# Adding the residual by transfers of GpSimd in the output product of a hybrid encoder block

## The chip, the cores and the metric

The kernel runs on one core of a Trainium2 chip. The metric is the device time of one execution in microseconds. A core has a matrix engine (TensorE, PE in the profile, with its weight loads as PEld), a vector engine (VectorE, DVE), a scalar engine (ScalarE, ACT), GpSimd (POOL) and SyncE (SP), which here only issues transfers. Each engine runs its own queue of instructions in order; semaphores hold an instruction back until what it needs is done. Transfers run on 16 DMA engines that all queues share.

## The reference

The computation is one layer of a hybrid encoder on 256 rows of 4096 numbers, all in float32. The parts that matter here are the last ones:

```
h = h + concat([y_a, y_c]) @ w_out                       # h was x, the input
gate = sigmoid(rms_norm(h, ple_norm_g) @ w_ple_gate + b_ple_gate)
h = h + gate * (p @ w_ple)
return rms_norm(h, final_g)
```

`y_a` (attention) and `y_c` (convolution) are the two halves of 2048 columns each. `rms_norm` divides a row by the root of its mean square, so it needs the sum of squares of each whole row of `h`. The kernel keeps `h` itself unscaled in the gate product and multiplies by the row's factor (`r_h` in the kernel) afterwards.

## The kernel before

The 256 rows are two halves of 128 (`h` = 0, 1 in the code), and the columns are eight blocks of 512. A product is computed for two column blocks at a time, which is called a group here: `w_out` has four groups, `w_ple_gate` has four. One group accumulates over 32 row blocks of the weights, two at a time, in 16 pairs. Every float32 operand is split into a high and a low part, and each product is three matrix products of TensorE (high by high, low by high, high by low), each 128 x 128 by 128 x 512. The high part of the weights is a cast on ScalarE (L204, `wh` or `uh`), the low part a subtraction on VectorE (L205, `wl` or `ul`). Tiles for the parts rotate through three buffers each, and weights (`wt`, 512 KB each, loaded by SyncE at L403) through five.

`mixed_product` treats some pairs in a plain manner (24 matrix products) and others in Strassen's manner with seven products for eight (21 matrix products, plus sums of weights, L426 to L431, on VectorE). A list of units gives the order of the pairs: `dense` is `1 0* 3 2* 5 4* ...`, where a star marks a pair done with seven products; `late` has all plain pairs of odd number first. The seven products need helper accumulators (`P1`, `P5`, `P6`, `P7`) in four PSUM banks beside the four accumulators `acc[h][j]`. After the last starred pair, `on_helpers` combines the helpers: `helper_sums` (L467 to L471) copies `P1` and makes three sums. After the last pair, the four quarters are finished from `acc`.

Work that can wait is put in a list, `later`. `fill(n)` takes `n` entries from it after each pair; `fills` sets `n` (2 in `w_out`, 4 in the gate product). `ahead` makes operands for the next product: `h_ahead` transposes finished blocks of `h` on TensorE (L170), splits them into high (L156, ScalarE) and low parts (L157, VectorE), and is called once before the last pair of `w_out` and then, pair by pair, in the first gate group.

A scheduler places the instructions: the order in the code gives priorities and the dependences, and each engine's queue is the scheduler's order, not the code's. Queues are in order on the chip.

In the output product, L1049 loads the two blocks of `x` into the tiles `hc` on SyncE's queue; these tiles are slots that the `y` blocks held before. `on_helpers` adds the helpers onto `hc` (L1057 to L1061), and L1070 adds the accumulators. `square_sum` (L500, ScalarE) sums the squares of each finished quarter through `later`. After the fourth group the list is emptied, and `rstd_of` (L504 and L138 on VectorE, L139 on GpSimd) makes `r_h`. Its first reader is L1091, in the `on_helpers` of the first gate group.

Of the kernel before, what the change touches and what calls it, by code (L numbers as in the profile page):

```python
# [10 lines left out]
F32 = mybir.dt.float32  # L11
F32R = mybir.dt.float32r
AF = mybir.ActivationFunctionType
ALU = mybir.AluOpType
AX = mybir.AxisListType

P = 128
NB = 512
# [7 lines left out]
def hybrid_block(  # L26
# [23 lines left out]
    nc = tc.nc  # L50
    _, T, D = x.shape
    NH = T // P
# [15 lines left out]
    def pool(name, bufs, stack=ctx, side=0, **kw):  # L68
        return stack.enter_context(tc.tile_pool(name=name, bufs=bufs, side=sides[side], **kw))

    cpool = pool("cpool", 1)
    act = pool("act", 8)
# [63 lines left out]
    def rsqrt(dst, src, n):  # L136

        nc.vector.tensor_scalar(dst, src, 1.0 / n, EPS, ALU.mult, ALU.add)  # L138
        nc.gpsimd.tensor_tensor(dst, dst, mhalf[:, : dst.shape[1]], ALU.pow)  # L139
# [40 lines left out]
    later = deque()  # L180

    def fill(n):
        for _ in range(min(n, len(later))):
            later.popleft()()
# [141 lines left out]

    def mixed_product(
        w, col, lhs, comb, order, on_helpers, ahead=None, fills=(0,), on_begin=None, apart=NB,
        left=(), begin=None,
    ):  # L330
# [64 lines left out]
        for n, (pair, seven) in enumerate(order):  # L395
# [59 lines left out]
            if n == last_seven:  # L455
                on_helpers(helper)
# [4 lines left out]
    tt, stt = nc.vector.tensor_tensor, nc.vector.scalar_tensor_tensor  # L461
    QUARTERS = ((0, 0), (1, 0), (0, 1), (1, 1))

    def helper_sums(helper, z):


        nc.scalar.copy(z[1][0], helper["P1"])  # L467
        tt(z[1][0], helper["P6"], z[1][0], ALU.add)
        tt(z[0][1], helper["P5"], z[1][0], ALU.add)
        tt(z[1][0], helper["P7"], z[1][0], ALU.add)  # L470
        tt(z[1][1], helper["P5"], z[1][0], ALU.add)  # L471

    def sum_tiles():

        t = [spool.tile([P, NH, NB], F32, tag="stage", name="z") for _ in range(2)]
        return t, [[t[j][:, h] for j in range(2)] for h in range(NH)]

    def scaled_pair(w, col, apart, order, r, fills, **kw):

        t, z = [], []  # L480

        def on_helpers(helper):
            for dst, src in zip((t, z), sum_tiles()):
                dst.extend(src)
            nc.scalar.activation(z[0][0], helper["P1"], AF.Identity, scale=r[:, :1])
            helper_sums(helper, z)
            for h, j in QUARTERS[1:]:
                nc.scalar.activation(z[h][j], z[h][j], AF.Identity, scale=r[:, h : h + 1])

        c = mixed_product(w, col, xT, xS, order, on_helpers, fills=fills, apart=apart, **kw)  # L490
        for h, j in QUARTERS:
            stt(  # L492
                z[h][j], c[h][j], r[:, h : h + 1], z[h][j],
                ALU.mult, ALU.subtract if j else ALU.add,
            )
        return t
# [5 lines left out]
    def rstd_of(partial, n, name):  # L502
        r = cpool.tile([P, partial.shape[1]], F32, name=name)
        nc.vector.tensor_reduce(r, partial, AX.X, ALU.add)  # L504
        rsqrt(r, r, n)
        return r
# [433 lines left out]
    for c0, order in zip(range(0, CW // NB, 2), point):  # L940
        row = broadcast_row(b_pw, c0 * NB, 2 * NB, tag="stage")
        rows = [row[:, j * NB : (j + 1) * NB] for j in range(2)]
        ys, z = [], []
# [4 lines left out]
        def on_helpers(helper):  # L948
            y_tiles()
            z.extend([ys[j][:, h, :] for j in range(2)] for h in range(NH))  # L950
            tt(z[0][0], helper["P1"], rows[0], ALU.add)
            helper_sums(helper, z)
            for h, j in QUARTERS[1:]:
                tt(z[h][j], z[h][j], rows[j], ALU.subtract if j else ALU.add)

        acc = mixed_product(w_pw[0], c0 * NB, uS, uC, order, on_helpers)
# [35 lines left out]
    def before_last(make):  # L992

        return lambda pair: make(0) if pair == dense[-1][0] else None
# [29 lines left out]
    hs, hT, hS = [], [], []  # L1024
# [17 lines left out]
                embedding()  # L1042

    ssq_h = cpool.tile([P, NH, D // NB], F32, name="ssq_h")
    for c0 in range(0, D // NB, 2):
        for j in range(2):
            hc = act.tile([P, NH, NB], F32, tag="act", name="hc")
            c = c0 + j
            nc.sync.dma_start(  # L1049
                hc, x[0, :, c * NB : (c + 1) * NB].rearrange("(h q) n -> q h n", q=P)  # L1050
            )
            hs.append(hc)

        def on_helpers(helper):
            _, z = sum_tiles()
            h00, h01, h10, h11 = (hs[c0 + j][:, h, :] for h in range(NH) for j in range(2))
            tt(h00, helper["P1"], h00, ALU.add)  # L1057
            helper_sums(helper, z)
            tt(h01, h01, z[0][1], ALU.subtract)
            tt(h10, h10, z[1][0], ALU.add)  # L1060
            tt(h11, h11, z[1][1], ALU.subtract)  # L1061

        acc = mixed_product(
            w_out[0], c0 * NB, yT, yS, dense if c0 else late, on_helpers,
            ahead=y_ahead if c0 == 0 else before_last(h_ahead) if c0 + 2 == D // NB else None,
            fills=(2,),
        )
        for h, j in QUARTERS:
            hc = hs[c0 + j][:, h, :]
            tt(hc, acc[h][j], hc, ALU.add)  # L1070
            later.append(partial(square_sum, ssq_h[:, h, c0 + j : c0 + j + 1], hc))
    fill(len(later))
    r_h = rstd_of(ssq_h, D, "r_h")


    n_f = D // NB
# [47 lines left out]
    c0 = n_f - 2  # L1124
    _, z = sum_tiles()
# [17 lines left out]
    def on_helpers(helper):  # L1143
# [4 lines left out]
    acc, add_left = mixed_product(  # L1148
        w_ple_gate[0], c0 * NB, hT, hS, final, on_helpers, fills=(4,), on_begin=on_begin,
        left=[None] * 3 + [kept] * 3,  # L1150
    )
# [119 lines left out]
```

## Time and profile before

| What | Value |
|---|---|
| Median of three runs | 2040.47 us (2038.33 to 2040.82) |
| Profiled execution | 2039.1 us, span 2037.3 us |
| Busy in the span | TensorE 2019.6 us, VectorE 1887.9, ScalarE 1200.8, GpSimd 8.1 |
| Bytes moved | 412.29 MB, 202 GB/s on average |
| Granted TensorE clock | 0.998 |

The span is the time from the first to the last instruction of the profiled execution, 1.8 us shorter than its device time. In the profile's views a line such as `L370 PE MATMUL acc<-wh,big_t 128*128 128x512 f32 x3788 | 1172.1, 391` names the source line, the engine, the operation, the output and the inputs, shapes and the count, and then the busy time in us and the mean of one in ns. In a timeline the first number is the start in us from the span's start, the second the duration, and in brackets stands the idle time of the engine ahead of the instruction with what ended it. Matrix products overlap in the pipeline, so the start to start distance says more than the duration. A row of the view by stretches gives for each engine the busy time and the number of instructions, then the granted clock, the busy share of the DMA engines and the GB/s that they moved.

### The profile page before, as it was taken

To read this page: it belongs to the slowest core of one execution; us is meant where nothing else is said; L and a number is where in the kernel's file an instruction comes from. 1 tells how busy PE (TensorE), PEld (TensorE's weight loads), DVE (VectorE), ACT (ScalarE), POOL (GpSimd) and SP (SyncE) were. 2 spreads that over 40 slices of the span, in tenths; PEclk is the share of its full clock that TensorE was granted. 3 is DMA by queue.
4 is the path that set the end of the run, shared out by engine and by line. 5 is a ranking of instruction groups with operands and counts; after the bars stand their busy time and mean duration, and the time that the engine had idled before them with its cause. 6 is when DMAs were issued, how large, how long until landed. Compare 5 with 4: busy or idle time off the path is not lost.

```text
span 2037.3 us, 26041 instructions
## 1 busy us (share of the span) xinstructions
PE 2019.6 (99%) x9106; PEld 1659.5 (81%) x9106; DVE 1887.9 (93%) x2688; ACT 1200.8 (59%) x1559; POOL 8.1 (0%) x19
## 2 busy tenths in 40 slices
PE   9999999999999999999999999999999999999997
PEld 7888888877888888888888888888888888888876
DVE  7999999799989998868899999999999999999998
ACT  7655546554565546676555656676565666655555
POOL 0000000000000000000000000000000000000000
PEclk9999999999999999999999999999999999999999
DMA  8666665666656665655666666676666656666765
GB/s 295 188 200 204 204 187 165 202 191 189 184 185 204 201 188 183 186 184 199 190 216 204 197 216 199 219 238 204 214 201 205 214 185 208 198 221 205 235 208 179
DMA packets 161853, 412.29 MB, mean 202 GB/s; under 512 B 12974, under 2 KB 16190, under 8 KB 161722
## 3 DMA queue, kind: packets, MB, share of 16 engines
q1 hardware_dynamic: 161072, 409.80, 63.3%
q8 instruction: 71, 1.16, 0.2%
q10 hardware_dynamic: 650, 0.84, 0.1%
q14 instruction: 60, 0.49, 0.1%
HBM read 406.39 MB, written 4.19 MB: 202 GB/s over the span
## 4 chain that ended last, share of the span: by engine, by line
PE 86%; DVE 10%; issue 2%; DMA 1%; ACT 1%; POOLq 0%; POOL 0%; ACTq 0%; DVEq 0%
PE acc L370 61%; PE acc_P L370 15%; PE acc L218 7%; DVE wl L205 4%; DVE cv L677 3%; DMA wt<-in_w_in_dram 1%; PE tmp_ps L170 1%; DVE ul L205 1%; PE tmp_ps L867 0%; PE tmp_ps L849 0%; ACT wh L204 0%; PE acc L358 0%; PE tmp_ps L834 0%; DVE z L492 0%; PE tmp_ps L872 0%
## 5 line engine op out<-in xcount | busy, mean ns | idle before, releaser
L370 PE MATMUL acc<-wh,big_t 128*128 128x512 f32 x3788 | 1172.1, 391 | 0.6 <-DVE z L988 0.3
L204 ACT CAST wh<-wt 128x1024 fp32r<-128x1024 f32 (+1 forms) x737 | 715.8, 982 | 543.0 <-PE acc L370 330.6
L205 DVE TENSOR_TENSOR wl<-wt,wh 128x1024 fp32r<-128x1024 f32 (+1 forms) x737 | 825.4, 1132 | 65.0 <-ACT wh L204 60.1
L370 PEld LDWEIGHTS acc<-wh,big_t 128*128 128x128 f32 x3788 | 708.4, 188 | 146.5 <-issue 0.6
L370 PE MATMUL acc<-wl,big_t 128*128 128x512 f32 x1894 | 731.1, 391 | 1.0 <-DVE wl L205 1.0
L370 PEld LDWEIGHTS acc<-wl,big_t 128*128 128x128 f32 x1894 | 355.2, 188 | 76.7 <-DVE wl L205 3.1
L677 DVE SCALAR_TENSOR_TENSOR cv<-uT,dw,cv 128x255 f32<-128x255 f32 (+23 forms) x480 | 204.9, 467 | 1.1
L204 ACT CAST uh<-ub 128x1024 fp32r<-128x1024 f32 x122 | 128.5, 1054 | 126.2 <-DVE ub L431 102.7
L218 PE MATMUL acc<-wh,big_t 128*128 128x512 f32 x560 | 173.1, 390 | 0.0
L204 ACT CAST uh<-ua 128x1024 fp32r<-128x1024 f32 x122 | 128.7, 1055 | 71.7 <-DVE ua L427 63.5
L205 DVE TENSOR_TENSOR ul<-ub,uh 128x1024 fp32r<-128x1024 f32 x122 | 149.0, 1221 | 8.8 <-ACT uh L204 7.8
L370 PE MATMUL acc_P<-uh,big_t 128*128 128x512 f32 x504 | 154.4, 392 | 0.0
L205 DVE TENSOR_TENSOR ul<-ua,uh 128x1024 fp32r<-128x1024 f32 x122 | 148.9, 1220 | 0.4 <-ACT uh L204 0.2
L218 PEld LDWEIGHTS acc<-wh,big_t 128*128 128x128 f32 x560 | 104.8, 188 | 21.4
L370 PEld LDWEIGHTS acc_P<-uh,big_t 128*128 128x128 f32 x504 | 93.3, 188 | 22.2 <-ACT uh L204 3.7
L218 PE MATMUL acc<-wl,big_t 128*128 128x512 f32 x280 | 109.1, 390 | 0.0
L426 DVE TENSOR_TENSOR ua<-wt 128x512 f32<-128x512 f32 x122 | 83.9, 688 | 25.9 <-DMA wt<-in_w_in_dram 19.0
L370 PE MATMUL acc_P<-ul,big_t 128*128 128x512 f32 x252 | 96.8, 392 | 0.0
L427 DVE TENSOR_TENSOR ua<-wt 128x512 f32<-128x512 f32 x122 | 83.7, 686 | 3.9 <-DMA wt<-in_w_in_dram 3.0
L431 DVE TENSOR_TENSOR ub<-ub,wt 128x512 f32<-128x512 f32 x122 | 83.8, 687 | 1.0
L430 DVE TENSOR_TENSOR ub<-ua,wt 128x512 f32<-128x512 f32 x122 | 83.7, 686 | 0.3
L370 PE MATMUL acc<-uh,big_t 128*128 128x512 f32 x244 | 75.4, 390 | 0.0
(241 smaller groups left out, 1523.0 us busy)
## 6 DMA issues: line engine op xcount, KB each, us to landing
wt<-in_w_in_dram SPq DMA_DIRECT2D x447, 512.0 KB, 4.0
wt<-in_w_out_dram SPq DMA_DIRECT2D x128, 512.0 KB, 4.2
wt<-in_w_ple_gate_dram SPq DMA_DIRECT2D x128, 512.0 KB, 4.2
wt<-in_w_pw_dram SPq DMA_DIRECT2D x32, 512.0 KB, 4.5
hc<-in_x_dram SPq DMA_DIRECT2D x8, 512.0 KB, 5.8
wt<-in_w_ple_dram SPq DMA_DIRECT2D x8, 512.0 KB, 4.2
xin<-in_x_dram SPq DMA_DIRECT2D x7, 512.0 KB, 8.2
out_dram<-hc SPq DMA_DIRECT2D x12, 256.0 KB, 2.4
```

The lines of the kernel that those rows point to most:

```text
L170: nc.tensor.transpose(pt[:, i * T + h * P : i * T + (h + 1) * P], src[:, h, b * P : (b + 1) * P], ident,)
L204: nc.scalar.copy(wh[:, :kc, :], wt[:, :kc, :]),
L205: nc.vector.tensor_tensor(wl[:, :kc, :], wt[:, :kc, :], wh[:, :kc, :].bitcast(F32), ALU.subtract),
L218: nc.tensor.matmul(acc, a, b[:, k, :], start=kb == 0 and kind == 0, stop=kb == kblocks - 1 and kind == 2,)
L370: nc.tensor.matmul(banks[name], a, b, start=name not in begun, stop=final and ends[name] == n and kind == 2 and not (left and name in "P2 ...
L426: plus(ua[:, 0], w0[:, 0], w0[:, 1])
L427: plus(ua[:, 1], w0[:, 1], w1[:, 1])
L430: plus(ub[:, 0], ua[:, 0], w1[:, 1])
L431: plus(ub[:, 1], ub[:, 0], w1[:, 0])
L677: nc.vector.scalar_tensor_tensor(cv[:, i, PAD - k :], uT[:, i, : T + k - PAD], dw[:, b, k : k + 1], cv[:, i, PAD - k :], ALU.mult, ALU.add,)
```

## The change

The residual `x` is no longer loaded ahead. `on_helpers` and the final additions write the product itself into the tiles `hc`: `P1` is copied there by ScalarE (L1053), `helper_sums` writes the other quarters there, and L1062 joins the accumulators. When both halves of a block are finished, a transfer issued by GpSimd (L1064) adds the block of `x` from DRAM onto the tile; there are eight such transfers of 512 KB. The squares go into `later` behind eight empty entries, so that at two entries for each pair they come four pairs later in the code. The list isn't emptied after the fourth group; the squares of its blocks, eight more empty entries and the making of `r_h` (`scale_h`) are taken from the list in the first gate group, four entries for each pair.

```diff
+    def x_columns(c):
+        return x[0, :, c * NB : (c + 1) * NB].rearrange("(h q) n -> q h n", q=P)
+
     for c0 in range(0, D // NB, 2):
-        for j in range(2):
-            hc = act.tile([P, NH, NB], F32, tag="act", name="hc")
-            c = c0 + j
-            nc.sync.dma_start(
-                hc, x[0, :, c * NB : (c + 1) * NB].rearrange("(h q) n -> q h n", q=P)
-            )
-            hs.append(hc)
+        hs.extend(act.tile([P, NH, NB], F32, tag="act", name="hc") for _ in range(2))
+        z = [[hs[c0 + j][:, h, :] for j in range(2)] for h in range(NH)]
 
         def on_helpers(helper):
-            _, z = sum_tiles()
-            h00, h01, h10, h11 = (hs[c0 + j][:, h, :] for h in range(NH) for j in range(2))
-            tt(h00, helper["P1"], h00, ALU.add)
+            nc.scalar.copy(z[0][0], helper["P1"])
             helper_sums(helper, z)
-            tt(h01, h01, z[0][1], ALU.subtract)
-            tt(h10, h10, z[1][0], ALU.add)
-            tt(h11, h11, z[1][1], ALU.subtract)
...
         for h, j in QUARTERS:
-            hc = hs[c0 + j][:, h, :]
-            tt(hc, acc[h][j], hc, ALU.add)
-            later.append(partial(square_sum, ssq_h[:, h, c0 + j : c0 + j + 1], hc))
-    fill(len(later))
-    r_h = rstd_of(ssq_h, D, "r_h")
+            tt(z[h][j], acc[h][j], z[h][j], ALU.subtract if j else ALU.add)
+        for j in range(2):
+            nc.gpsimd.dma_start(hs[c0 + j], x_columns(c0 + j), accum_op=ALU.add)
+        later.extend([lambda: None] * 8)
+        for h, j in QUARTERS:
+            later.append(partial(square_sum, ssq_h[:, h, c0 + j : c0 + j + 1], z[h][j]))
+    r_h = cpool.tile([P, NH], F32, name="r_h")
+
+    def scale_h():
+        nc.vector.tensor_reduce(r_h, ssq_h, AX.X, ALU.add)
+        rsqrt(r_h, r_h, D)
+
+    later.extend([lambda: None] * 8 + [scale_h])
```

## The prediction

> **What bounds the kernel now.** I read the page first, then busy times by stretch, then TensorE's timeline.
>
> ```profile
> span 2037.3 us, 26041 instructions
> PE 2019.6 (99%) x9106; PEld 1659.5 (81%) x9106; DVE 1887.9 (93%) x2688; ACT 1200.8 (59%) x1559; POOL 8.1 (0%) x19
> ```
>
> ```profile
> core 0: us, PE busy (x) PEld busy (x) DVE busy (x) ACT busy (x) POOL busy (x), PEclk, DMA share, GB/s
> 1312.00:1360.00 48.00, 48.00 (x241) 40.17 (x240) 44.72 (x82) 33.53 (x57) 0.00 (x0) 1.00 0.70 225
> ```
>
> ```profile
> 1664.00:1668.40 4.40, 4.40 (x26) 3.77 (x26) 4.10 (x9) 3.86 (x11) 0.00 (x0) 1.00 0.01 4
> ...
> 1412.00:1660.00 248.00, 248.00 (x1104) 205.50 (x1103) 237.81 (x283) 149.91 (x180) 0.00 (x0) 1.00 0.63 206
> ```
>
> The w_out product, which the change touches, runs from about 1312 to 1663. Between 1412 and 1660 TensorE is busy 248.00 of 248.00 us, VectorE 237.81 and ScalarE 149.91. A busy TensorE may still hide small waits, so I look at its starts:
>
> ```profile
> 1416.51 0.61 PE L370 MATMUL acc<-wh,big_t 128*128 128x512 f32 x2
> ...
> 1421.95 0.61 PE L370 MATMUL acc_P<-wh,big_t 128*128 128x512 f32 x2
> ...
> 1426.72 0.62 PE L370 MATMUL acc<-wh,big_t 128*128 128x512 f32 x2
> 1427.17 0.39 PE L370 MATMUL acc<-wl,big_t 128*128 128x512 f32 x1
> ```
>
> At 1416.51 the second group of w_out begins. Its first pair of row blocks is plain, 24 products; it ends at 1421.95, so one product takes 5.44/24 = 0.227 us. The second pair, with 21 products, ends at 1426.72: again 0.227. There are no hidden waits; TensorE alone sets the pace here, and its products are the same after the change. So work taken from VectorE in this stage buys nothing. TensorE's 17.7 us without work (2037.3 - 2019.6) lie elsewhere.
>
> **What is removed.** 16 additions on VectorE (four lines, each once for each of four groups) and eight loads in SyncE's queue:
>
> ```profile
> L1049 SPq DMA_DIRECT2D hc<-in_x_dram x8: 368/379/386, 1320.0 to 1364.6; - x8
> ...
> L1057 DVE TENSOR_TENSOR hc<-acc_P,hc x4: 682/683/692, 1402.7 to 1646.7; 128x512 f32<-128x512 f32 x4
> ```
>
> The view of hc's instructions shows one of the four lines (the three others are additions of the same shape). 16 x 0.683 = 10.9 us of VectorE, all beside a TensorE that does not wait: gain 0. The loads lie between weights from 1320 to 1365; in the stretch 1312 to 1360 TensorE is busy 48.00 of 48.00 us with them there: gain 0. If a short wait of VectorE in the other stages went too, that would be under a microsecond.
>
> **What is added on ScalarE.** One copy of P1 in each group, ahead of the copy that was there:
>
> ```profile
> 1647.60 0.57 ACT L467 COPY z<-acc_P 128x512 f32<-128x512 f32 x1
> ```
>
> 4 x 0.57 = 2.3 us on an engine that is idle for 98 us in 248. The helper banks are read 0.57 us later. Their next writer is the P1 product, at 1421.95 in the group shown; the last read there was at 1409.26:
>
> ```profile
> 1409.26 0.68 DVE L471 TENSOR_TENSOR z<-acc_P,z 128x512 f32<-128x512 f32 x1
> ```
>
> 12 us cover it: cost 0. If that cover went, 0.57 us for each group.
>
> **The eight adding transfers.** Each waits on GpSimd for its block's two last additions. Behind them in GpSimd's queue stands only the power of r_h, whose first reader is L1091:
>
> ```profile
> L1091 DVE SCALAR_TENSOR_TENSOR z<-acc_P,r_h,row x3: 747/747/751, 1738.8 to 1914.8; 128x512 f32<-128x512 f32 x3
> ```
>
> The factor would be done near 1680, 58 us ahead: cost 0. The transposes of the last two blocks are also late enough:
>
> ```profile
> L170 PE MATMUL tmp_ps<-ident,hc x64: 270/272/273, 1655.9 to 1701.2; 128*128 128x128 f32 x64
> ```
>
> The last of them starts at 1701.2 and the pair before about 6.4 us earlier, 25 us after the sums: cost 0.
>
> The squares are the point. In the program they come four pairs later, but the scheduler has moved them forward again. ScalarE's queue in the changed program reads, at the start of the second group:
>
> ```
> L204 TensorCopy wh_12393<-wt_12375    (second pair)
> L500 Activation <-hc_11514            (square, block 0, upper)
> L500 Activation <-hc_11514            (square, block 0, lower)
> L500 Activation <-hc_11515            (square, block 1, upper)
> L204 TensorCopy wh_12428<-wt_12424    (third pair)
> ```
>
> The first square waits for the first transfer, the third for the second; the high part of the third pair's weights stands behind them, and behind that its low part on VectorE, on which TensorE waits. Nothing excuses a late transfer. The deadline is from these rows:
>
> ```profile
> 1415.14 2.48 DVE L1070 TENSOR_TENSOR hc<-acc,hc 128x512 f32<-128x512 f32 x4
> ...
> 1422.59 0.69 DVE L426 TENSOR_TENSOR ua<-wt 128x512 f32<-128x512 f32 x1 [0.37 <-DMA wt<-in_w_out_dram]
> 1423.20 1.22 DVE L205 TENSOR_TENSOR wl<-wt,wh 128x1024 fp32r<-128x1024 f32 x1
> ```
>
> ```profile
> 1415.86 0.63 ACT L500 ACTIVATE junk<-hc 128x512 bf16<-128x512 f32 x1
> 1416.39 0.19 ACT L500 ACTIVATION_READ_ACCUMULATOR junk<-hc 128x1 f32 x1
> ...
> 1421.92 1.06 ACT L204 CAST wh<-wt 128x1024 fp32r<-128x1024 f32 x1 [1.66 <-PE acc L370]
> ```
>
> TensorE wants the third pair's low part at 1427.17. Back from it: 1.22 for the low part, 1.06 for the cast, 0.82 for the third square: the second transfer must have landed by 1424.1. Its inputs are done at 1415.14 + 2.48 = 1417.6, those of the first near 1416.4. So 6.5 us are allowed.
>
> How long does such a transfer take? No row shows one, so it is bounded by loads of the same size and by GpSimd's nearest instruction:
>
> ```profile
> DMA packets 865, 2.56 MB, mean 321 GB/s; under 512 B 76, under 2 KB 76, under 8 KB 865
> ...
> q1 hardware_dynamic: 865, 2.56, 92.0%
> ```
>
> ```profile
> DMA to landing us min/median/max: 3.4/4.2/5.5
> ```
>
> ```profile
> 1669.02 0.69 POOL L139 TENSOR_TENSOR r_h<-r_h,mhalf 128x2 f32<-128x2 f32 x1 [667.58 <-DVE r_h L138]
> ```
>
> The first fence is the DMA view from 1358 to 1366, where loads are queued: 321 GB/s at 92% busy is 349 GB/s full, 1.5 us for 512 KB. The second is the landing of w_out's weights from 1412 to 1660; the shortest, 3.4 to 3.6, is 1.5 of transfer and 2.0 fixed. Lower bound: an adding transfer costs what a load costs. Then the second lands at 1416.4 + 0.7 (GpSimd) + 1.5 + 1.5 + 1.5 (one weight tile between) + 2.0 = 1423.6, half a microsecond early: 0. A gain isn't possible, since TensorE isn't waiting. Estimate taken: it must fetch the tile as well as x, so twice the bytes and 3.0 us each: 1426.6, late by 2.5 us. Upper bound: three times, and two weight tiles between: 1416.4 + 0.7 + 9.0 + 3.0 + 2.0 = 1431.1, late by 7.0. I take the middle, since reading two operands for one result is certain and a third factor isn't.
>
> At three of the four group ends (blocks 0 to 5) this costs 3 x 2.5 = 7.5 us. The fourth end, before the gates, has another order: the first square stands there ahead of the high parts of hT on ScalarE, and VectorE's low parts of these stand ahead of the low part for the second pair's second half.
>
> ```profile
> 1664.37 1.28 DVE L1070 TENSOR_TENSOR hc<-acc,hc 128x512 f32<-128x512 f32 x2
> ...
> 1670.37 0.88 DVE L157 SCALAR_TENSOR_TENSOR big_t<-tmp_ps,prm,big_t 128x256 fp32r<-128x256 f32 x2
> ```
>
> ```profile
> 1669.18 0.83 ACT L156 ACTIVATE big_t<-tmp_ps,prm 128x256 fp32r<-128x256 f32 x2
> ```
>
> ```profile
> 1673.00 0.39 PE L370 MATMUL acc<-wl,big_t 128*128 128x512 f32 x1
> ```
>
> TensorE wants that part at 1673.0; less 1.22, 0.88, half of 0.83 and 0.82 the first transfer must land by 1669.7. Its inputs are done near 1665.0, and the DMA engines are empty until 1668.4 (share 0.01): 1665.0 + 0.7 + 3.0 + 2.0 = 1670.7, late by 1.0 (0 at the lower bound, 2.5 at the upper).
>
> **Sum.** 7.5 + 1.0 = 8.5 us on the profiled execution's 2039.1 (span 2037.3 and 1.8 around it) gives 2047.6. The median 2040.47 is 1.4 above that execution, so 2049.0. The upper bounds give 21.0 + 2.5 = 23.5, 2064; the lower 2040.5.
>
> **Rivals.** *In time (not slower).* Adding costs no more than loading, the second transfer lands at 1423.6 and the first of the last end at 1665.0 + 0.7 + 1.5 + 2.0 = 1669.2; nobody waits: 2040.5. It decides where the second transfer lands within 6.5 us of its inputs and the last end's first within 4.7. For it: weights land in 4.2 at the median. Against it: it leaves 0.5 us. The Trainium skill, DMA: Bandwidth & Descriptors, section on the anatomy of a DMA on the GpSimd path, gives 2.0 us plus bytes over 436 GB/s, an estimate of 3.2 us for 512 KB, which would be this rival; no row here shows a transfer of GpSimd, and the 3.4 of SyncE's loads agrees.
>
> *GpSimd is held up by VectorE.* If GpSimd can start a transfer only where VectorE pauses, the first start in the second group is the 0.37 us pause that ends at 1422.59. Then 1422.2 + 0.7 + 6.0 + 1.5 + 2.0 = 1432.4, late by 8.3, and 3 x 8.3 = 25 us with some 10 at the last end, where the next pause ends at 1676.37:
>
> ```profile
> 1676.37 1.23 DVE L205 TENSOR_TENSOR wl<-wt,wh 128x1024 fp32r<-128x1024 f32 x1 [0.80 <-ACT wh L204]
> ```
>
> That is 2075. Against it: the power of r_h (its row is above) ran on GpSimd in 0.69 us with VectorE busy beside it. The Trainium skill, SBUF — State Buffer, section "Who interferes with whom", lets a two-input tensor_tensor hold up only GpSimd's reads, and blames copies for starving such transfers; VectorE's rows in this stage are TENSOR_TENSOR, so by it this rival is unlikely.
>
> *Faster.* VectorE's relief would have to end waits of TensorE. The starts every 0.227 us leave none; 0.2% would be 4.1 us.
>
> **How the numbers follow.** Late transfers, 2044.6 to 2062: 0.46. In time, within 4.1 us: 0.36. Held up, or adding dearer than three loads, above 2062: 0.14. Faster by over 4.1 us: 0.04. The bound 0.2% is 4.1 us, about what a measurement of this kernel can tell from no change (its three runs span 2.5). Slower is then 0.60. The forecast is 2049; the range 2039.5 to 2062 holds the first two cases, 0.8. The likeliest case's own range is 2044.6 to 2062.
>
> **What would show it.** Late: in the second to fourth groups a ScalarE square of hc waits for a DMA, and TensorE has a gap of 1 to 4 us once in each, 10 us after the group's start; GpSimd's transfers land 7 us or more after the last addition. In time: squares without idle ahead of them, landing in under 6 us. Held up: landing only after VectorE's pauses. The forecast is wrong too if a gap opens elsewhere, for instance where VectorE's L426 waits longer than 0.37 us for weights that share the DMA engines.

## The result, and the profile after

The changed kernel takes 2071.48 us (median of five runs, 2069.65 to 2074.58), 1.0157 times the kernel before (95% interval 1.0143 to 1.0170): 31.0 us slower. The profiled execution took 2071.35 us with a span of 2069.6; against the span before, 2037.3, that is 32.3 us to be found. The lines of the page that answer to those shown of before, with its part on the DMA queues and its line on GpSimd's transfers:

```profile
span 2069.6 us, 26035 instructions
PE 2029.9 (98%) x9106; PEld 1663.7 (80%) x9106; DVE 1878.7 (91%) x2672; ACT 1200.0 (58%) x1563; POOL 18.0 (1%) x27
...
q1 hardware_dynamic: 158896, 405.60, 61.8%
q0 software_dynamic: 2176, 4.19, 1.3%
...
hc<-in_x_dram POOLq DMA_DIRECT2D x8, 512.0 KB, 6.2
```

TensorE has the same 9106 instructions and is 10.3 us longer at them; 22 us more are idle. The waits of TensorE in the changed kernel (columns: total, times, longest, in us) name the idle part:

```profile
PE acc L370 <- ACT wh L204: 18.1, 4, 6.2
PE tmp_ps L170 <- DMA pin<-in_p_dram: 1.8, 1, 1.8
...
PE acc L370 <- DVE wl L205: 1.3, 1, 1.3
```

18.1 us are waits for a cast of ScalarE: one long wait in each of the second to fourth groups. ScalarE's timeline at the first of them shows what the cast stands behind; GpSimd's timeline shows when the transfers were issued:

```profile
1419.07 1.05 ACT L204 CAST wh<-wt 128x1024 fp32r<-128x1024 f32 x1 [2.50 <-DVE wl L205]
1422.98 0.63 ACT L500 ACTIVATE junk<-hc 128x512 bf16<-128x512 f32 x1 [2.85 <-DMA hc<-in_x_dram]
...
1430.96 0.63 ACT L500 ACTIVATE junk<-hc 128x512 bf16<-128x512 f32 x1 [6.50 <-DMA hc<-in_x_dram]
...
1431.59 1.97 ACT L204 CAST wh<-wt 128x1024 fp32r<-128x1024 f32 x2
```

```profile
1417.06 1.37 POOL L1064 DMA_DIRECT2D hc<-in_x_dram  x1 [415.81 <-DVE hc L1062]
1423.16 1.24 POOL L1064 DMA_DIRECT2D hc<-in_x_dram  x1 [4.73 <-issue]
```

The first square waits until 1422.98 for the first transfer, the third until 1430.96 for the second, and only then come the third pair's casts. GpSimd issues the second transfer 6.1 us after the first, when the first has landed. The DMA view of three stretches (packets, MB, busy share of the 16 engines) shows in which order the engines serve what is asked for (shares are of each short stretch, with packets counted where they start, so one can be over 100%):

```profile
q0 software_dynamic: 229, 0.47, 104.4%
issues: line engine op xcount, KB each, median us to landing
wt<-in_w_out_dram SPq DMA_DIRECT2D x3, 512.0 KB, 6.1
...
q1 hardware_dynamic: 341, 1.27, 99.6%
issues: line engine op xcount, KB each, median us to landing
hc<-in_x_dram POOLq DMA_DIRECT2D x1, 512.0 KB, 7.7
...
q0 software_dynamic: 220, 0.42, 73.1%
```

From 1419.2 to 1422.0 the engines serve GpSimd's queue alone, although three weight tiles are asked for by then (at 1419.10, 1419.70 and 1421.97); from 1422.6 to 1425.8 they serve those weights alone, although the second transfer is asked for at 1423.16; from 1427.2 to 1430.4 they serve that one. Not all of this is waiting for the other queue: by the packets' records the first transfer too moved its first packet 2.1 us after its issue, and a weight tile that found the engines idle in the kernel before 1.0 us after its own. The first of the three tiles took 3.0 us to its first packet, the second transfer 2.9, so they were held up for some 2.0 and 0.8 us. In this stretch the bytes thus moved in the order of asking; a run below shows that it isn't always so.

The long waits cost more than their length. In the view by stretches (same columns as in the prediction) the granted clock after the first wait is 0.52 for 5 us:

```profile
1426.40:1432.60 6.20, 0.34 (x2) 0.00 (x0) 0.00 (x0) 1.64 (x4) 0.00 (x0) 0.85 0.48 88
1432.70:1437.80 5.10, 5.06 (x12) 3.53 (x13) 5.10 (x6) 3.05 (x5) 0.00 (x0) 0.52 0.55 170
1440.00:1450.00 10.00, 10.00 (x46) 8.29 (x45) 10.00 (x13) 5.66 (x7) 0.00 (x0) 1.00 0.55 176
```

In the second stretch TensorE is "busy" throughout, with 12 products in 5.10 us instead of the 22 that 0.227 us each would give. The clock is down for about 6.8 us at each of the three waits, from a point within the wait:

```profile
1430.70:1437.60 6.90, 4.89 (x11) 3.40 (x12) 4.95 (x6) 4.79 (x8) 0.00 (x0) 0.51 0.38 117
1522.90:1529.70 6.80, 5.61 (x12) 3.97 (x13) 5.67 (x7) 4.23 (x8) 0.00 (x0) 0.50 0.47 140
1611.70:1618.50 6.80, 3.48 (x7) 2.33 (x8) 3.54 (x5) 4.28 (x8) 0.00 (x0) 0.50 0.24 52
```

What is left of it when TensorE goes on differs: 4.9, 5.7 and 3.5 us of slow products. The 32.3 us come together as follows. The first three rows add up what the distances between starts of products exceed 0.227 us by; the fourth compares the starts of products of the same number in the two kernels.

| Place | Excess, us |
|---|---|
| Three waits for the third pair's cast | 6.1 + 6.4 + 5.6 = 18.1 |
| Slow products right behind them | 2.6 + 3.0 + 2.0 = 7.6 |
| Three short waits elsewhere (at 1416.3, 1507.4 and 1642.1) | 0.43 + 0.74 + 1.03 = 2.2 |
| Fourth end and first gate group | 4.0 |
| Rest | 0.4 |
| Sum | 32.3 |

### The profile page after: what moved, and what is told of

Read it like the earlier page. It is cut to its first block, busy times and chain, and to the rows that moved or that the text cites. A ratio compares the mean times of both kernels' runs of the same rounds, so it can differ in the third digit from the quotient of the medians.

```text
span 2069.6 us, 26035 instructions
## 1 busy us (share of the span) xinstructions
PE 2029.9 (98%) x9106; PEld 1663.7 (80%) x9106; DVE 1878.7 (91%) x2672; ACT 1200.0 (58%) x1563; POOL 18.0 (1%) x27
## 3 DMA queue, kind: packets, MB, share of 16 engines
q1 hardware_dynamic: 158896, 405.60, 61.8%
## 4 chain that ended last, share of the span: by engine, by line
PE 76%; DVE 15%; DMA 4%; issue 3%; ACT 1%; POOLq 0%; ACTq 0%; POOL 0%; DVEq 0%
PE acc L370 52%; PE acc_P L370 14%; PE acc L218 7%; DVE wl L205 6%; DVE cv L677 4%; DVE ul L205 1%; DMA wt<-in_w_in_dram 1%; DMA hc<-in_x_dram 1%; PE tmp_ps L170 1%; DMA wt<-in_w_out_dram 1%; ACT wh L204 1%; DVE z L492 0%; DVE ua L427 0%; DVE hc L1062 0%; DVE ub L430 0%
## 5 line engine op out<-in xcount | busy, mean ns | idle before, releaser
L370 PE MATMUL acc<-wh,big_t 128*128 128x512 f32 x3788 | 1177.7, 393 | 18.9 <-ACT wh L204 18.1
L426 DVE TENSOR_TENSOR ua<-wt 128x512 f32<-128x512 f32 x122 | 83.7, 686 | 41.2 <-DMA wt<-in_w_in_dram 20.3
```

The source lines that it names most:

```text
L370: nc.tensor.matmul(banks[name], a, b, start=name not in begun, stop=final and ends[name] == n and kind == 2 and not (left and name in "P2 ...
L426: plus(ua[:, 0], w0[:, 0], w0[:, 1])
```

## The experiments

Ratios are to the kernel before, run on the same chip beside each kernel; its medians there were 2038.9 to 2039.5 us.

**More room for GpSimd's descriptors.** The question was whether the first transfer's descriptors fill the room and so hold back the issue of the second, and whether that late issue is what costs.

```diff
-dynamic_dma_scratch_size=1024
+dynamic_dma_scratch_size=2048
```

> The changed kernel with one number altered: the room that GpSimd has for the descriptors of its transfers, 2048 bytes per partition in place of 1024. Every queue's order is the same. Theory 'room' (the second of two adding transfers waits on GpSimd because the first one's descriptors fill the room): the second transfer is issued within 1.5 us of the first, lands some 3 us earlier, TensorE's wait on the third pair's cast shrinks from about 6 us to 1 to 3 us at each of three group ends, and the time falls from 2071 to 2046 to 2056 us. Theory 'in turn' (GpSimd takes adding transfers one after the other whatever the room): the second is still issued about 6 us after the first, 2071 us.

Measured: 2069.56 us, 1.0151 (1.0136 to 1.0166). GpSimd's timeline now has both transfers in one row:

```profile
1416.41 2.62 POOL L1064 DMA_DIRECT2D hc<-in_x_dram  x2 [415.24 <-DVE hc L1062]
```

The second is issued right behind the first, so the room did hold it back; but it lands at 1429.67 (1430.86 in the changed kernel), and TensorE still waits 17.9 us for casts. That the late issue costs the time falls. The three weight tiles were asked for behind the second transfer here (1418.43 to 1421.31, against 1417.59), and yet the two queues share the engines about half and half from 1423.0 to 1428.5, the stretch of these lines:

```profile
q0 software_dynamic: 259, 0.51, 54.7%
q1 hardware_dynamic: 284, 1.04, 49.5%
```

So the order of asking isn't always the order of serving; when it is was not settled.

**Transfers that copy instead of adding.**

```diff
-            nc.gpsimd.dma_start(hs[c0 + j], x_columns(c0 + j), accum_op=ALU.add)
+            nc.gpsimd.dma_start(hs[c0 + j], x_columns(c0 + j))
```

> The changed kernel with GpSimd's transfers copying x over the tile in place of adding it, so the product of w_out is left out of h. Theory 'room': a copy needs about half as many descriptors, two fit, the second is issued within 1.5 us, each moves in about half the time (packets of 2048 bytes take about 90 ns in place of 178 ns), and the time is 2040 to 2046 us. Theory 'in turn': the second is issued only when the first has landed, some 5 us later, lands near 11 us after the sums, and the time is 2048 to 2060 us.

Measured: 2055.06 us (one run). The transfers are issued 1.2 us apart, as the first theory says, but the time that goes with it is missed. The second transfer lands at 1425.67 instead of 1430.86, the waits in front of the third pair are 1.7 to 2.0 us instead of 6, and the clock stays at 1.00. By the changed kernel's page, eight adding transfers take 1.3% of 2069.6 us, 3.4 us of the engines each, and 405.60 MB of plain ones 61.8%, 1.65 us for 512 KB: adding costs twice the engines' time here.

**Squares held behind the casts.** Each square is tied behind the cast of the pair at which `later` gives it out, so that the scheduler can't move it forward; in the fourth group they come eight entries later.

```diff
-            later.append(partial(square_sum, ssq_h[...], z[h][j]))
+            later.append(partial(late_square, ssq_h[...], z[h][j]))   # square_sum, behind last_cast
```

> The changed kernel with the squares really four pairs late: each is tied behind the last cast of the pair at which it is taken from the list (in the fourth group, two pairs later still), so that no square stands ahead of the third pair's cast. The transfers and their room are as in the changed kernel. Theory 'the squares ahead of the cast': TensorE's waits of about 6 us and the slow products after them go, 2040 to 2045 us. Rival 'the transfers themselves': weights that share the DMA engines with the adding transfers still come late for VectorE, and 5 us or more of the 31 stay, 2046 to 2060 us.

> The squares held as in the kernel before this one and the room doubled. If the squares ahead of the cast are the whole path, the same as with the squares held alone within 2 us. If the two transfers back to back crowd out weights more than when they come one after the other, 1 to 5 us slower than with the squares held alone.

Measured: 2048.80 us, 1.0052 (1.0037 to 1.0067), and with the larger room as well 2047.60, 1.0044 (1.0027 to 1.0061). 22.7 of the 31 us go with the place of the squares alone. There is no wait over 2 us and no slow clock any more, and the waits at the fourth end are gone too. Left are short waits of TensorE on VectorE, which itself waits for weights; TensorE's waits from 1410 to 1730, and VectorE's timeline:

```profile
PE acc L373 <- DVE wl L207: 4.4, 5, 1.4
PE acc L373 <- DVE hc L1072: 1.1, 2, 0.9
```

```profile
1425.19 0.69 DVE L429 TENSOR_TENSOR ua<-wt 128x512 f32<-128x512 f32 x1 [3.77 <-DMA wt<-in_w_out_dram]
1425.80 2.36 DVE L207 TENSOR_TENSOR wl<-wt,wh 128x1024 fp32r<-128x1024 f32 x2
```

**The moved squares without transfers.** In the kernel before, only the squares and the factor are placed as in the change.

> One part alone, on the kernel before: the loads of x by SP and VectorE's four additions stay as they were, only the squares come four pairs later and the scaling factor of h is made in the first gate group. The theory so far (the squares cost time only because they wait for an adding transfer in front of a cast) says that here they wait for nothing, since their input is ready at the end of a group: the time of before, 2036 to 2044 us. If the moved squares or the moved factor cost time by themselves, the rival, a part of the 31 us must show here: 2045 us or more.

Measured: 2039.28 us, 1.0002 (0.9992 to 1.0011). In ScalarE's queue the squares of the first group run from 1415.57 to 1418.94 there, about where they were before (1415.86 to 1419.24), and not between the casts of the second and the third pair as in the changed kernel. So the run shows that the later place in the list and the later factor cost nothing; what the changed kernel's place in the queue would cost with the input there was not tried.

**Where the last 9 us come from: three misses.** Four transfers of 256 KB instead of two of 512, two pairs apart:

```diff
-            nc.gpsimd.dma_start(hs[c0 + j], x_columns(c0 + j), accum_op=ALU.add)
...
+                later.append(partial(add_x, z[h][j], x_columns(c0 + j)[:, h, :]))   # behind last_cast
+                later.extend([lambda: None] * 3)
...
```

> The changed kernel with the squares held behind the casts as in the run before (2048.8), and the two adding transfers of 512 KB of the first three pairs of blocks cut into four of 256 KB, each tied behind a cast two pairs of weights (about 11 us) after the last; the fourth pair of blocks as in the change. If the 8 to 9 us that were left come from the weights' transfers being crowded within the 12 us in which 1 MB is added, they go: 2040 to 2044 us, and no weight tile of this place takes over 6 us. If the adding costs its share wherever it stands, the rival, 2046 to 2050 us.

Measured: 2050.59 us, 1.0058 (1.0043 to 1.0073): no better. Now the held kernel with transfers that copy:

> The held squares again, but GpSimd's transfers copy x over the tile and add nothing: the product of w_out is left out of h, so this is a measurement of time alone. If the time on the DMA engines is what delays the weights, a transfer that takes half of it leaves about half of the 9 us or less: 2041 to 2045 us. If it is GpSimd's queue beside SP's queue, whatever the transfer does, the rival, 2047 to 2050 us as with the adding.

Measured: 2050.53 us, 1.0056 (1.0039 to 1.0073): the adding isn't the cause of what is left. (Some 1.7 us of it are one fall of the clock, shown in the last section; without it the time would be about that of the adding kernel.) Next, the kernel before with the x of its second to fourth group loaded at this place, and not at 1320 to 1365 us:

```diff
+            added = tt(hc, acc[h][j], hc, ALU.add)
...
+        if c0 + 2 < D // NB:
+            load_x(nc.gpsimd, added)    # x's next two blocks, behind `added`; nc.sync in the second run
```

> The kernel before with nothing of the change but the place of the loads: x's blocks of the second to fourth group of w_out are loaded not at 1320 to 1365 us but by GpSimd right after the last addition of the group before (two plain transfers of 512 KB at about 1418, 1508 and 1599 us), a whole group ahead of their use. If the 9 to 10 us that stay with the squares held come from 1 MB being moved at a place where VectorE waits for each weight tile, they are here too: 2047 to 2051 us. If they come from the adding, the copy on ScalarE or the order of VectorE's work in the changed kernel, the rival, 2038 to 2042 us.

> The same moved loads of x, issued by SP among its weight tiles. If the engines' time at that place is the cause, whichever queue asks for it, 2046 to 2051 us again, as with GpSimd. If it is that a GpSimd transfer goes ahead of weight tiles while SP would have it take its turn behind them, 2038 to 2043 us.

Measured: 2041.27 us, 1.0011 (1.0001 to 1.0020) by GpSimd and 2039.31, 1.0005 (0.9996 to 1.0014) by SP. Moving the bytes to this place isn't enough by itself: in both, the value that goes with that theory missed.

**No transfers, and small ones.** The held kernel without its transfers has the same order of instructions on TensorE, VectorE, ScalarE and SP:

```diff
-        for j in range(2):
-            nc.gpsimd.dma_start(hs[c0 + j], x_columns(c0 + j), accum_op=ALU.add)
```

> The held squares with GpSimd's eight transfers left out, so that x is not added to h at all, and the order of every instruction on TensorE, ScalarE, VectorE and SP as in the run that gave 2048.8: a measurement of time alone. If the 9 us that stay are the transfers' packets standing ahead of weight tiles, nothing stays: 2038 to 2042 us. If the new order on VectorE and ScalarE costs by itself (the copy of P1, the subtraction into the block, the accumulators that are read later), it stays at 2046 to 2050 us. In between, 2042 to 2046 us, both have a share, and the difference to 2048.8 is that of the transfers.

Measured: 2040.05 us, 1.0006 (0.9996 to 1.0015). The whole of what was left belongs to the transfers; the new order by itself costs nothing. VectorE's row that waited 3.77 us in the held kernel, here:

```profile
1421.60 0.69 DVE L429 TENSOR_TENSOR ua<-wt 128x512 f32<-128x512 f32 x1 [1.09 <-DMA wt<-in_w_out_dram]
1422.20 2.35 DVE L207 TENSOR_TENSOR wl<-wt,wh 128x1024 fp32r<-128x1024 f32 x2
```

Then the transfers in pieces of 64 KB, in two groups and in all three:

```diff
...
+            for q in range(0, P, 32):
+                for h, j in QUARTERS:
+                    later.append(partial(
+                        add_x, z[h][j][q : q + 32, :], x_columns(c0 + j)[q : q + 32, h, :]
+                    ))
...
```

> The held squares, with the two adding transfers of the first two pairs of blocks cut into sixteen of 64 KB (32 partitions of one quarter), one to each pair of weights of the following group; the third pair of blocks in four of 256 KB and the fourth as in the change. If a transfer costs what it shifts the weight tiles behind it by, and VectorE can take up a few tenths, most of the 6 us that the second and third group lost go: 2043 to 2046 us. If every byte moved here costs its time on the engines, the rival, 2049 to 2052 us.

> The held squares with the transfers of the first three pairs of blocks all in pieces of 64 KB: one to each pair of weights in the second and third group, two to each pair in the fourth. In the run with pieces of 64 KB for two groups the third pair of blocks, in four pieces of 256 KB, still cost 5 us in the fourth group. If the length of one transfer ahead of a weight tile is what costs, the fourth group loses 1 to 2 us instead: 2043 to 2046 us. If the bytes or the order cost, 2047 to 2050 us as before.

Measured: 2047.68 us, 1.0043 (1.0027 to 1.0060), a miss, and 2044.06, 1.0026 (1.0016 to 1.0036), as expected if the length of a transfer is what costs. The small pieces are also spread over a whole group, one or two to each pair; length and spacing were not tried apart. With small pieces throughout, TensorE is busy without a break in the stretch in which the held kernel had its first waits (its row first, then that of the small pieces):

```profile
1418.00:1430.00 12.00, 11.73 (x52) 9.33 (x51) 8.23 (x11) 4.73 (x5) 1.24 (x1) 1.00 0.96 257
```

```profile
1418.00:1430.00 12.00, 12.00 (x55) 9.94 (x54) 9.57 (x13) 5.86 (x7) 0.77 (x1) 1.00 0.82 265
```

Beside these stand the landings of the first weight tile issued after a group's last additions, relative to the start of the third pair's first product (all from the records of the first group that has a transfer behind it; the issue and landing of the tile, in us):

| Kernel | issued | landed |
|---|---|---|
| before | -7.9 | -4.2 |
| held, no transfers | -7.6 | -3.7 |
| held, pieces of 64 KB | -7.5 | -3.5 |
| held, pieces of 256 KB | -7.5 | -0.9 |
| held, adding 512 KB | -7.6 | -1.1 |
| held, copying 512 KB | -7.6 | -0.6 |
| before, moved loads by GpSimd | -8.8 | -4.1 |
| before, moved loads by SP | -8.2 | -2.4 |

In the three held kernels with a transfer of 256 KB or more in front of it, the tile lands 2.7 to 3.1 us later than in the held kernel without transfers. A first tile that starts late also shares the engines with the two tiles asked for behind it, which would be why 256 KB delay it about as much as 512; that was not tried by itself. Why the moved loads cost next to nothing was not settled: with GpSimd the first tile was issued half a microsecond after the transfer and slipped through; with SP it landed 1.8 us later than before and nothing waited, since VectorE's queue there has the low parts ahead of L426. That is read from the traces and was not tried by itself. Nor was it shown where the 4 us sit that small pieces still cost.

**A cast held up without any transfer of GpSimd,** in the kernel before, to see whether the slow clock follows from standing still.

```diff
+        first = [square_sum(unused, wt[:, 0, :]) for _ in range(slow.pop() if slow else 0)]
         made = (
             nc.scalar.copy(wh[:, :kc, :], wt[:, :kc, :]),
...
-            fills=(2,),
+            fills=(2,), delay=(0, 6, 9, 12)[c0 // 2],
```

> The kernel before with one cast of the weights held up on purpose in each of the last three groups of w_out, by 6, 9 and 12 needless squares of the landed tile ahead of it (0.63 us each by the changed kernel's rows: 3.8, 5.7 and 7.6 us), in the fifth pair. No transfer of GpSimd is there. If TensorE's clock falls because TensorE stood still for long, the gaps of some 1 to 3, 3 to 5 and 5 to 7 us show it in order: the granted clock stays 1.00 behind the shortest and falls to about 0.5 for some 5 us behind the longest, and the sum is 2050 to 2062 us. If the slow clock behind the 6 us waits came with the adding transfers, the rival, it stays 1.00 behind all three and the time is 2045 to 2055 us, by the gaps alone.

> The held-up cast again in the kernel before, with 14, 18 and 24 needless squares (8.8, 11.3 and 15.1 us); the run with 6, 9 and 12 showed that some 7 us of it are covered. Gaps of about 2, 4 and 8 us follow in TensorE. If the clock falls because TensorE stood still, without any transfer of GpSimd near, the products behind the longest take about 0.43 us for some 5 us, and those behind the shortest 0.23. If the slow clock belongs to the adding transfers, the rival, 0.23 us behind all three.

Measured: 2047.66 us with 6, 9 and 12 squares (one run): the waits are covered but for gaps of 0.4 to 0.7 us, so the first run says nothing of the clock. Some 3 of its 8.6 us are many small delays (from 1312 to 1663, 512 of 1554 starts are 231 to 245 ns behind the one before, against 74 of 1586 in the kernel before); what makes them was not tried. With 14, 18 and 24 squares, 2073.47 us (one run). Its stretches in and behind the three waits:

```profile
1442.40:1445.30 2.90, 1.59 (x6) 1.10 (x7) 1.16 (x2) 2.87 (x6) 0.00 (x0) 1.00 0.00 0
1445.40:1448.70 3.30, 3.30 (x9) 2.59 (x8) 1.71 (x2) 0.65 (x2) 0.00 (x0) 0.50 0.67 195
1530.00:1534.70 4.70, 0.48 (x1) 0.16 (x1) 0.00 (x0) 4.54 (x13) 0.00 (x0) 0.94 0.00 0
1534.80:1540.80 6.00, 5.96 (x13) 4.29 (x14) 2.94 (x3) 1.91 (x3) 0.00 (x0) 0.50 0.60 190
1622.10:1631.30 9.20, 0.46 (x1) 0.14 (x1) 0.00 (x0) 8.85 (x25) 0.00 (x0) 0.54 0.00 0
1631.40:1636.40 5.00, 4.96 (x11) 3.47 (x12) 3.16 (x4) 1.42 (x2) 0.00 (x0) 0.50 0.52 160
```

The granted clock is 0.50 behind all three, for 3.3, 6.0 and 5.0 us, with no transfer of GpSimd in the stage. So the slow clock comes with TensorE's waits and needs no transfer. It came even behind the shortest (0.7 and 1.6 us of wait, one product apart), where the expectation had full speed.

## Why the prediction was wrong

The direction was right, the size was not: 2049.0 was forecast, 2039.5 to 2062 as the range, and 2071.48 came. The parts above add up to 32.3 us where the prediction had 8.5. Of the 23.8 us between them, 10.6 are the waits' length, 7.6 the slow products behind them, 3.0 the fourth end and 2.6 the short waits and the rest.

- *TensorE sets the pace, so relief of VectorE gains nothing; the copy on ScalarE and GpSimd's queue cost nothing.* Right: the held kernel without transfers has the relief and the copy, and takes the time of before (1.0006). In the changed kernel the factor is done at 1712.8, 58 us ahead of its first reader at 1771.0.
- *The loads' removal gains nothing.* Right, but half a step. Their other half, that the same bytes now go to a stage where weights land just before they are used, was not costed. It is worth the 9 us that stay with the squares held. In the changed kernel itself it hides behind the longer waits for the casts: L426 waits there for weights too, but TensorE waits longer for ScalarE. The last sentence of the prediction named this very place (VectorE's L426), as a doubt only.

```profile
1425.32 0.69 DVE L426 TENSOR_TENSOR ua<-wt 128x512 f32<-128x512 f32 x1 [3.38 <-DMA wt<-in_w_out_dram]
```

- *The squares stand ahead of the third pair's cast, and the third waits for the second transfer.* Right in place and mechanism: ScalarE's rows above show it, and tying the squares behind the casts takes 22.7 us away.
- *The second transfer lands at 1426.6.* This term was mis-sized: 1430.86. Twice the bytes was the right reading (3.4 us of the engines each, 3.0 taken). "One weight tile between" was not: three stood between, 1.65 us each. The prediction's own form with these sizes, 1416.4 + 0.7 + 6.8 + 5.0 + 2.0, gives 1430.9. All three are issued before the second transfer, and their bytes moved between the two; the issues in the trace of before (1418.78, 1419.38 and 1422.29) would have given the count. The waits came to 18.1 us instead of 7.5, within the upper bound of 21.0. The Trainium skill, DMA: Bandwidth & Descriptors, section on the anatomy of a DMA, gave an estimate of 3.2 us; the two transfers landed 5.8 and 7.7 us after their issue, the first with the engines to itself from 1419.2 to 1422.0, so it doesn't hold for these transfers that add.
- *A wait of TensorE costs its length.* This is the step that failed outright: the text never mentions the clock behind a wait. The three waits of about 6 us leave 4.9, 5.7 and 3.5 us at half the clock behind them, which costs 7.6 us. The stated range ended 9.5 us too low, at 2062, although the prediction's own upper bounds add up to 2064; without the slow products the time would be about there. The Trainium skill, TensorE: Matmul & The Clock Gate, Part 1, says that the clock halves after an idle window of some 3.4 us and comes back after a busy one. The trace agrees in kind (6.1 us of wait, then 0.52 for 5.1 us), but not on the idle time that it takes: in the third wait the clock fell 2.2 us after the end of TensorE's last product, and in one other run a wait of 2.0 us was enough.
- *The fourth end costs 1.0 us, 2.5 at most.* It cost 4.0: 1.5 at 1700.6, for the low part that the prediction named, and 2.0 at 1739.2, where TensorE waits for `pin`, whose load stands later in SP's queue (issued at 1737.5 instead of 1704.5). The order of SP's queue at this place was not looked at. Both go with the squares held, whose order has that load early again (1712.5).
- *The rivals.* "In time" fell with the landing. "Held up by VectorE" had a time near the result, 2075, and is wrong: GpSimd issues at 1417.06 while VectorE goes from one instruction to the next, and what delays the second issue goes away with more room for descriptors. "Faster" falls with the kernel without transfers, which has all of VectorE's relief and takes the time of before.

No version ran faster than the kernel before; the best that adds x by transfers took 2044.06.

## What to carry to other kernels

Ahead of giving an in-order engine an operation on a transfer's result, count everything that is asked of the DMA engines before that transfer and while it waits, and look at what stands behind the operation in the queue the scheduler really made: an entry "four pairs later" in the code may stand next. A wait on a saturated TensorE is priced with its length and with the slow clock behind it; here it was 7.6 us on top of 18.1. A load that is free where nobody waits for weights need not be free at another place: look at how early the neighbouring tiles land before moving it, and cut it into pieces if it must go there.

## What the runs showed of the hardware

- TensorE's clock fell to half after a wait of 2.0 us in one place (the held kernel with copying transfers, by stretches: 9 products in 3.30 us), and stayed at 1.00 behind waits of 1.7 to 2.0 us in another run. In waits of 4.6 to 9.1 us it fell every time, eight waits in three runs, before TensorE went on. In the records of the clock each slow stretch lasts 3.4, 6.8 or 13.7 us: 6.8 at all three waits of the changed kernel, 3.4, 6.8 and 13.7 at those of the longer delays.

```profile
1510.60:1512.70 2.10, 0.34 (x2) 0.00 (x0) 1.80 (x3) 0.62 (x1) 0.00 (x0) 1.00 0.22 88
1513.10:1516.40 3.30, 3.30 (x9) 2.63 (x8) 3.30 (x5) 1.05 (x1) 0.00 (x0) 0.50 0.77 252
```

- An adding transfer occupies the DMA engines twice as long as a load: 178 ns for a packet of 2048 bytes, against 84 ns for one in the moved loads of x by SP (medians of the packets' records).
- With the kernel's room for descriptors, one adding transfer of 512 KB fills it: the second was issued 6.1 us later, and 1.2 us later with twice the room. Copying transfers of the same size, with half as many and larger packets, were issued 1.2 us apart in the smaller room.
